# State-space input tables computed in place from turned inputs and factor rows, with their transfers begun by GpSimd

## The chip, the cores and the metric

The kernel runs as one program on one core of one Trainium2 chip. The metric is the device time of one execution in microseconds (us), and lower is better. TensorE is called PE, VectorE DVE, ScalarE ACT, GpSimd POOL and SyncE SP, as the profile does. A name such as L884 is a line of the kernel file.

## The reference

One layer of a decoder trunk is computed for 256 tokens of width 2048, in float32: a SwiGLU feed-forward block, a mixer made of a state-space part (S5) and a sparse attention part, and a second feed-forward block. The part that the change touches is the preparation of the S5 parameters:

```
dt = exp(log_dt);  lam = min(a_re, -1e-4) + i a_im
ab = exp(lam * dt)                      # one complex factor per state
co = (ab - 1) / lam                     # zero-order hold
bb = co * b                             # input matrix
x[t] = ab * x[t-1] + bb u[t]            # scan over the tokens
y[t] = Re(c x[t]) + d * u[t]
```

There are 64 groups of 16 channels with 64 states each. The kernel treats 4 tokens at a time: it needs, for every state, the products of ab^3, ab^2, ab and 1 with bb (the input table), the products of ab to ab^4 with c (the output table), and the 4 by 4 triangle of direct responses of one token to a later one (the third part of the output table). These tables depend on weights alone.

## The kernel before

The first feed-forward block (`ffn`, called with `tables`) multiplies the activations by gate and up weights in 11 blocks of 512 columns. The first five blocks (0 to 4) take both halves apart by plain products, and from block 5 on another scheme with fewer products is used (lines L523 to L525, tile `bank`). Each weight tile `raw` (128x1024, 512 KB) is loaded by SP, rounded by ACT into `hi` (L103), and the rest `lo` is formed by DVE (L105). PE then makes three products from the parts of weight and activation (`hi,ah` L278, `lo,ah` L279, `hi,al` L280), for two token tiles: 12 matmuls for one `raw`, and 192 for one half of a block. There are four `hi` and four `lo` buffers and four accumulators `acc`. A finished gate half is read by ACT (silu, L690, into `wk`), which frees its accumulators for the next half; DVE multiplies by the up half (L691).

The table work, `s5_tables`, hides beside these blocks. A list `background` holds its steps: `s5_params` (some 90 small DVE operations on 128x32 and two sines on ACT), `bias_table` (a relative-position table of the attention: ACT loads `wk<-in_rel_bias`, POOL fills it, ACT stores `rb_one` and spreads it as `rb`, 3 MB), and for each of eight channel tiles ct the steps `loads`, three `b_power`, `into`, four `c_power` and `out_of`. Function `pump` takes steps off the list as blocks go on. A scheduler then orders the instructions of every engine from these steps and their dependences, by its own estimate of times; on the chip each engine runs its row in that fixed order.

For one ct before the change: ACT begins the loads `ld` of b and c; DVE forms `bd` = co*b (L851 to L853) and three powers of it (L860 to L862); PE turns the result by 8 transposes (L322, tile `xp`, through `transpose4`), ACT copies it out (L875, tile `bt`) and begins its store to `s5in` (L876). DVE forms the powers of c in `gb` (L854, L855, L867 to L869). In `out_of` PE multiplies `bd` by `gb` (L884), DVE takes the result to `hs` (L887, L888), POOL spreads it by 16 small copies into `hz` (L892), and ACT begins the stores of `gb` and `hz` to `s5out` (L895, L896). `ld`, `bd`, `gb` and `bt` have one buffer each, so `gb` of the next ct waits until the store of this one has landed. After ct 7 the space of these tiles is given to the tiles of the second scheme, among them `sh` (written by ACT at L496), so `sh` waits for the last store of `hz`.

Of the kernel before, what the change touches and what calls it, by code (L numbers as in the profile page):

```python
# [10 lines left out]
F32 = mybir.dt.float32  # L11
F32R = mybir.dt.float32r
I32 = mybir.dt.int32
AF = mybir.ActivationFunctionType
ALU = mybir.AluOpType
# [158 lines left out]
def body(tc, a):  # L174
    nc = tc.nc
    V, S, G, T = nc.vector, nc.scalar, nc.gpsimd, nc.tensor
# [5 lines left out]
    dp = es.enter_context(tc.tile_pool(name="scratch", bufs=1, space=DRAM))  # L182
# [80 lines left out]
    background = []  # L263
# [54 lines left out]
    def transpose4(src, cols=128, n=4):  # L318
        pool = spare[0]
        p = pool.tile([128, n, 128], F32, name="xp", tag=pool.name)  # L320
        for k in range(n):
            last_transpose[0] = T.transpose(p[:, k, :], src[:, k * cols:(k + 1) * cols], ident).ins  # L322
        return p
# [296 lines left out]
    def ffn(name, rr, gen, post, last, tables=False):  # L620
# [9 lines left out]
        if tables:  # L630
            pre[0] = tc.tile_pool(name="pre", bufs=1, reuse_waits="tile")
            with tc.issue_after(stream.rounded[9]):
                s5_tables(pre[0].__enter__())
# [102 lines left out]
    ar = cp.tile([128, 32], F32, name="ar")  # L736
    ai2 = cp.tile([128, 2, 32], F32, name="ai2")
    cor = cp.tile([128, 32], F32, name="cor")
    coi2 = cp.tile([128, 2, 32], F32, name="coi2")
# [81 lines left out]
    def bc(x, ct, two):  # L821
        x = x[:, :, 4 * ct:4 * ct + 4] if two else x[:, 4 * ct:4 * ct + 4].unsqueeze(1).to_broadcast([128, 2, 4])
        return x.unsqueeze(3).to_broadcast([128, 2, 4, 32])


    in_dram = dp.tile([8, 128, 1024], F32, name="s5in")
    out_dram = dp.tile([8, 128, 1536], F32, name="s5out")

    def s5_tables(sp_):
        dsk = sp_.tile([128, 8], F32, name="dsk")  # L830
        nc.scalar.dma_start(dsk, a["ssm_d"])
        hzs = [sp_.tile([128, 4, 128], F32, name=f"hz{i}") for i in range(2)]
        for z in hzs:
            G.memset(z, 0.0)
        fold = sp_.tile([128, 32], F32, name="fold")
        V.tensor_copy(fold, ident[:, 0:32])
        for q in range(1, 4):
            V.tensor_tensor(fold, fold, ident[:, 32 * q:32 * q + 32], op=ALU.add)
        t12 = sp_.tile([128, 2, 2, 4, 32], F32, name="t12")
        t1, t2 = t12[:, 0], t12[:, 1]  # L840
        state = {}

        def loads(ct):
            for nm in ("b", "c"):
                w = sp_.tile([128, 2, 4, 32], F32, name="ld", tag="ld" + nm, bufs=1)
                nc.scalar.dma_start(w.rearrange("p r q c -> p (r q c)"), a["ssm_" + nm][ct])
                state[nm] = w
            state["bd"] = sp_.tile([128, 2, 4, 4, 32], F32, name="bd")
            state["gb"] = sp_.tile([128, 2, 4, 5, 32], F32, name="gb")
            b0, bd, gb = state["b"], state["bd"], state["gb"]  # L850
            V.tensor_tensor(t1, b0, bc(cor, ct, False), op=ALU.mult)  # L851
            V.tensor_tensor(t2, b0[:, ::-1], bc(coi2, ct, True), op=ALU.mult)
            V.tensor_tensor(bd[:, :, :, 3, :], t1, t2, op=ALU.add)  # L853
            V.tensor_copy(gb[:, 0, :, 0, :], state["c"][:, 0])  # L854
            V.tensor_scalar(gb[:, 1, :, 0, :], state["c"][:, 1], -1.0, None, op0=ALU.mult)  # L855

        def b_power(ct, j):
            bd = state["bd"]
            src = bd[:, :, :, j + 1, :]
            V.tensor_tensor(t1, src, bc(ar, ct, False), op=ALU.mult)  # L860
            V.tensor_tensor(t2, src[:, ::-1], bc(ai2, ct, True), op=ALU.mult)
            V.tensor_tensor(bd[:, :, :, j, :], t1, t2, op=ALU.add)  # L862

        def c_power(ct, k):
            gb = state["gb"]
            src = gb[:, :, :, k - 1, :]
            V.tensor_tensor(t1, src, bc(ar, ct, False), op=ALU.mult)  # L867
            V.tensor_tensor(t2, src[:, ::-1], bc(ai2, ct, True), op=ALU.mult)
            V.tensor_tensor(gb[:, :, :, k, :], t1, t2, op=ALU.subtract)  # L869

        def into(ct):
            bt = sp_.tile([128, 2, 512], F32, name="bt")
            for r in range(2):
                p = transpose4(state["bd"][:, r].rearrange("p q j c -> p (q j c)"))
                S.activation(bt[:, r], p, AF.Copy)  # L875
            nc.scalar.dma_start(in_dram[ct], bt.rearrange("p r s -> p (r s)"))  # L876

        def out_of(ct):
            bd, gb = state["bd"], state["gb"]
            hz = hzs[ct % 2]  # L880
            hp = xp.tile([128, 4, 32], F32, name="xp", tag="xp")
            for q in range(4):
                for r in range(2):
                    T.matmul(hp[32 * q:32 * q + 32], bd[:, r, q, 3, :],  # L884
                             gb[:, r, q, 0:4, :], start=r == 0, stop=r == 1, tile_position=(0, 32 * q))
            hs = sp_.tile([128, 4, 32], F32, name="hs")
            V.scalar_tensor_tensor(hs[:, 0, :], fold, dsk[:, ct:ct + 1], hp[:, 0, :], op0=ALU.mult, op1=ALU.add)  # L887
            V.tensor_copy(hs[:, 1:, :], hp[:, 1:, :])  # L888
            hq = hz.rearrange("p q (i c) -> p q i c", i=4)
            for q in range(4):  # L890
                for j in range(4):
                    G.tensor_copy(hq[32 * j:32 * j + 32, q, j:, :], hs[32 * q:32 * q + 32, 0:4 - j, :])  # L892
            od = out_dram[ct].rearrange("p (r q k) -> p r q k", r=3, q=4)
            for r in range(2):
                nc.scalar.dma_start(od[:, r], gb[:, r, :, 1:5, :].rearrange("p q k c -> p q (k c)"))  # L895
            nc.scalar.dma_start(od[:, 2], hz)  # L896

        start = stream.rounded[7]

        def at_start(f):  # L900
            with tc.issue_after(start):
                f()

        background.append(lambda: at_start(s5_params))
        background.append(bias_table)
        for ct in range(8):
            background.append(lambda ct=ct: loads(ct) if ct else at_start(lambda: loads(0)))
            for j in (2, 1, 0):
                background.append(lambda ct=ct, j=j: b_power(ct, j))
            background.append(lambda ct=ct: into(ct))  # L910
            for k in range(1, 5):
                background.append(lambda ct=ct, k=k: c_power(ct, k))
            background.append(lambda ct=ct: out_of(ct))
# [510 lines left out]
def _block_diag(x):  # L1424
    z = np.zeros((8, 2, 64, 4, 2, 16), x.dtype)
    x = x.reshape(8, 4, 2, 64, 16)
    for gp in range(2):
        z[:, gp, :, :, gp, :] = x[:, :, gp].transpose(0, 2, 1, 3)
    return z.reshape(8, 128, 4, 32)


def layout(i):
    f = {k: np.asarray(v) for k, v in i.items()}
    f = {k: (v if k in ("x", "rel_bias") else v[0]) for k, v in f.items()}
    d = {"x": np.ascontiguousarray(f["x"][0])}
# [4 lines left out]
    for n in ("ffn1", "ffn2"):  # L1440
# [3 lines left out]
    w = f["w_in"]  # L1444
    cut = np.cumsum([0, 1024, 1024] + [256] * 6 + [48, D, D])
    ssm, q, kc, vc, ks, vs, kw, vw, gn, ga, gb = (w[:, cut[j]:cut[j + 1]] for j in range(11))
    heads = [(2 * (p // 4) + hf) * 4 + p % 4 for p in range(8) for hf in range(2)]
    q = q.reshape(D, 16, 64)[:, heads].reshape(D, 1024)
# [14 lines left out]
    d["ssm_p"] = np.ascontiguousarray(np.stack([st(f["ssm_a_re"]), st(f["ssm_a_im"]), st(dt)], axis=1))  # L1463
    d["ssm_b"] = np.ascontiguousarray(np.stack(
        [_block_diag(f["ssm_b_re"]), _block_diag(f["ssm_b_im"])], axis=2)).reshape(8, 128, 256)
    d["ssm_c"] = np.ascontiguousarray(np.stack(
        [_block_diag(f["ssm_c_re"].transpose(0, 2, 1)), _block_diag(f["ssm_c_im"].transpose(0, 2, 1))],
        axis=2)).reshape(8, 128, 256)
# [20 lines left out]
```

## Time and profile before

| what | value |
|---|---|
| median of 3 runs | 2117.07 us (2113.35 to 2119.12) |
| profiled execution | 2120.92 us, its span 2119.2 us |
| PE busy | 2096.6 us (99%) |
| DVE busy | 1572.3 us (74%) |
| ACT busy | 1115.5 us (53%) |
| POOL busy | 273.3 us (13%) |
| bytes moved | 437.63 MB, mean 207 GB/s |

A busy time is the time in which at least one instruction of the engine runs; consecutive matmuls overlap, so their distance is shorter than the duration that is shown for one. The instructions that begin a transfer are not counted as busy and are shown with the name of the engine's queue (ACTq, SPq). The table work lies between about 20 and 250 us of the span.

### The profile page before, as it was taken

The numbers are of one execution on the slowest core, as the hardware profiler recorded it, in microseconds if no ns is written. First come the engines' busy times: TensorE is split into PE (matmuls) and PEld (weight loads), VectorE is DVE, ScalarE is ACT, GpSimd is POOL, SyncE is SP. The second block draws the span as 40 slices with busy tenths as digits, with TensorE's granted clock in tenths as the row PEclk, the third lists the DMA queues.
The fourth block names the chain that finished last, engine by engine and source line by source line (L and its number), as shares of the span: only waits on it lengthen the run. The fifth ranks groups of instructions, "written<-read, shape, count | busy, mean of one in ns | idle before, by whom it ended". The sixth has DMA issues, their size and how long they took to land.

```text
span 2119.2 us, 27930 instructions
## 1 busy us (share of the span) xinstructions
PE 2096.6 (99%) x10048; PEld 1726.9 (81%) x10048; DVE 1572.3 (74%) x2268; ACT 1115.5 (53%) x1537; POOL 273.3 (13%) x494
## 2 busy tenths in 40 slices
PE   8999999999999999999999999999999999999998
PEld 7887788888888878998787778888878888888886
DVE  7898788886867864454456656577898889778676
ACT  6444455555555565554445554465555555555453
POOL 1222300000000002993104320000000000000000
PEclk9999999999999999999999999999999999999999
DMA  8877656565665766567754346676556665656665
GB/s 285 268 239 234 202 196 211 197 213 180 205 206 198 272 205 225 163 223 248 276 165 139 122 144 214 203 268 184 188 191 197 208 197 190 219 170 210 217 207 179
DMA packets 137146, 437.63 MB, mean 207 GB/s; under 512 B 14880, under 2 KB 27312, under 8 KB 136880
## 3 DMA queue, kind: packets, MB, share of 16 engines
q1 hardware_dynamic: 117504, 403.10, 58.0%
q10 hardware_dynamic: 19504, 32.75, 4.5%
q8 instruction: 79, 1.29, 0.2%
q14 instruction: 59, 0.48, 0.1%
HBM read 417.42 MB, written 21.52 MB: 207 GB/s over the span
## 4 chain that ended last, share of the span: by engine, by line
PE 81%; POOL 8%; DVE 5%; issue 2%; DMA 2%; ACT 1%; ACTq 0%; DVEq 0%; SPq 0%; POOLq 0%
PE bank L524 15%; PE bank L525 15%; PE bank L523 15%; PE acc L278 10%; PE acc L279 10%; PE acc L280 10%; DVE lo L105 2%; POOL st L1005 2%; POOL sc L1002 2%; PE xp L322 2%; POOL sc L1003 1%; POOL st L1004 1%; DMA raw<-in_ffn_gu 1%; POOL hz L892 1%; DMA s5out<-gb 1%
## 5 line engine op out<-in xcount | busy, mean ns | idle before, releaser
L105 DVE TENSOR_TENSOR lo<-raw,hi 128x1024 fp32r<-128x1024 f32 (+3 forms) x676 | 796.7, 1186 | 353.7 <-ACT hi L103 352.2
L103 ACT ACTIVATE hi<-raw 128x1024 fp32r<-128x1024 f32 (+3 forms) x676 | 686.1, 1023 | 682.1 <-PE acc L280 306.8
L278 PE MATMUL acc<-hi,ah 128*128 128x512 f32 (+2 forms) x1072 | 414.9, 388 | 2.0 <-ACT hi L103 1.9
L279 PE MATMUL acc<-lo,ah 128*128 128x512 f32 (+2 forms) x1072 | 413.9, 386 | 0.0
L280 PE MATMUL acc<-hi,al 128*128 128x512 f32 (+2 forms) x1072 | 412.6, 385 | 0.0
L524 PE MATMUL bank<-lo,ah 128*128 128x512 f32 x758 | 296.7, 391 | 2.3 <-DVE lo L105 2.3
L525 PE MATMUL bank<-hi,al 128*128 128x512 f32 x746 | 290.7, 390 | 0.0
L523 PE MATMUL bank<-hi,ah 128*128 128x512 f32 x758 | 282.0, 391 | 0.0
L278 PEld LDWEIGHTS acc<-hi,ah 128*128 128x128 f32 x1072 | 201.4, 188 | 42.8 <-ACT hi L103 2.7
L279 PEld LDWEIGHTS acc<-lo,ah 128*128 128x128 f32 x1072 | 201.7, 188 | 38.9 <-issue 2.1
L280 PEld LDWEIGHTS acc<-hi,al 128*128 128x128 f32 x1072 | 201.6, 188 | 38.3 <-DVE al L351 0.3
L524 PE MATMUL bank<-lo,hT 128*128 128x512 f32 x520 | 202.5, 389 | 0.0
L525 PE MATMUL bank<-hi,hT 128*128 128x512 f32 x520 | 202.3, 389 | 0.0
L523 PE MATMUL bank<-hi,hT 128*128 128x512 f32 x520 | 190.7, 390 | 0.1
L524 PEld LDWEIGHTS bank<-lo,ah 128*128 128x128 f32 x758 | 142.4, 188 | 32.5 <-DVE lo L105 3.5
L523 PEld LDWEIGHTS bank<-hi,ah 128*128 128x128 f32 x758 | 142.3, 188 | 29.3
L525 PEld LDWEIGHTS bank<-hi,al 128*128 128x128 f32 x746 | 140.1, 188 | 28.7
L103 ACT ACTIVATE hi<-sums 128x1024 fp32r<-128x1024 f32 x84 | 88.5, 1054 | 63.0 <-DVE sums L140 29.7
L523 PEld LDWEIGHTS bank<-hi,hT 128*128 128x128 f32 x520 | 97.5, 188 | 21.1 <-ACT hi L103 0.9
L524 PEld LDWEIGHTS bank<-lo,hT 128*128 128x128 f32 x520 | 97.6, 188 | 20.2
L525 PEld LDWEIGHTS bank<-hi,hT 128*128 128x128 f32 x520 | 97.6, 188 | 20.1
L105 DVE TENSOR_TENSOR lo<-sums,hi 128x1024 fp32r<-128x1024 f32 x84 | 101.0, 1217 | 3.9 <-ACT hi L103 3.1
(322 smaller groups left out, 2674.3 us busy)
## 6 DMA issues: line engine op xcount, KB each, us to landing
raw<-in_ffn_gu SPq DMA_DIRECT2D x352, 512.0 KB, 4.3
raw<-in_ffn_d SPq DMA_DIRECT2D x176, 512.0 KB, 4.3
raw<-in_w_ya SPq DMA_DIRECT2D x64, 512.0 KB, 3.4
raw<-in_w_in SPq DMA_DIRECT2D x40, 512.0 KB, 4.1
raw<-in_w_gate_b SPq DMA_DIRECT2D x32, 512.0 KB, 3.7
raw<-in_w_out SPq DMA_DIRECT2D x32, 512.0 KB, 3.8
raw<-in_w_o SPq DMA_DIRECT2D x16, 512.0 KB, 3.9
tab<-s5out ACTq DMA_DIRECT2D x8, 768.0 KB, 6.5
```

The lines of the kernel that those rows point to most:

```text
L103: self.rounded.append(nc.scalar.activation(h, r, AF.Copy).ins)
L105: self.rest = nc.vector.tensor_tensor(l, r, h.bitcast(F32), op=ALU.subtract).ins
L278: T.matmul(o, lh, wh[:, k, :], start=kk + k == 0, stop=False)
L279: T.matmul(o, lh, wl[:, k, :], start=False, stop=False)
L280: last_product[0] = T.matmul(o, ll, wh[:, k, :], start=False, stop=kk + k == nk - 1).ins
L322: last_transpose[0] = T.transpose(p[:, k, :], src[:, k * cols:(k + 1) * cols], ident).ins
L523: T.matmul(out, lh, wh[:, j, :], start=key not in self.started, stop=False)
L524: T.matmul(out, lh, wl[:, j, :], start=False, stop=False)
L525: last_product[0] = T.matmul(out, ll, wh[:, j, :], start=False, stop=last).ins
L892: G.tensor_copy(hq[32 * j:32 * j + 32, q, j:, :], hs[32 * q:32 * q + 32, 0:4 - j, :])
L1002: G.tensor_tensor(w[:, 0], x, a4r2, op=ALU.mult)
L1005: G.tensor_tensor(y, y, w[:, 1], op=ALU.add)
```

## The change

`b_power` and the transposes of `into` go. Instead, a new step `coefs` right after `s5_params` multiplies co by ab three times (18 small DVE operations and two copies on 128x32), turns the four results by two PE transposes, and ACT copies them to three rows of 128x128 (real part, imaginary part with both signs), which POOL stores to a new DRAM tile `s5k`. A new input `ssm_bt` holds b already turned and repeated four times, so that its rows are already those of the input table. For each ct, `loads` now also loads this (`bt0`, 512 KB) and four stretches of `s5k`, each spread over 32 partitions (`kt`, 32x1536, 192 KB each). `into` is two halves of three DVE operations on 128x512: a product with the real factor, a product of the other half with the imaginary factor, and their sum. `bd` keeps only co*b, for `out_of`. All transfers of the tables (`dsk`, `ld`, `bt0`, `kt`, `s5k`, `s5in`, `s5out`) are begun by POOL instead of ACT: 11 for one ct.

```diff
     out_dram = dp.tile([8, 128, 1536], F32, name="s5out")
+    k_dram = dp.tile([128, 384], F32, name="s5k")
     def s5_tables(sp_):
         dsk = sp_.tile([128, 8], F32, name="dsk")
-        nc.scalar.dma_start(dsk, a["ssm_d"])
+        G.dma_start(dsk, a["ssm_d"])
         hzs = [sp_.tile([128, 4, 128], F32, name=f"hz{i}") for i in range(2)]
...
         state = {}
+        def coefs():
+            w = work().rearrange("p (r j c) -> p r j c", r=4, j=4)
+            k, t = w[:, 0:2], w[:, 2:4]
+            tt = V.tensor_tensor
+            V.tensor_copy(k[:, 0, 3], cor)
+            V.tensor_copy(k[:, 1, 3], coi2[:, 1])
+            for j in (2, 1, 0):
+                xr, xi = k[:, 0, j + 1], k[:, 1, j + 1]
+                tt(t[:, 0, 0], xr, ar, op=ALU.mult)
+                tt(t[:, 0, 1], xi, ai2[:, 1], op=ALU.mult)
+                tt(k[:, 0, j], t[:, 0, 0], t[:, 0, 1], op=ALU.subtract)
+                tt(t[:, 0, 2], xr, ai2[:, 1], op=ALU.mult)
+                tt(t[:, 0, 3], xi, ar, op=ALU.mult)
+                tt(k[:, 1, j], t[:, 0, 2], t[:, 0, 3], op=ALU.add)
+            p = transpose4(k.rearrange("p r j c -> p (r j c)"), n=2)
+            rows = work().rearrange("p (v s) -> p v s", v=4)
+            S.activation(rows[:, 0], p[:, 0], AF.Copy)
+            S.activation(rows[:, 1], p[:, 1], AF.Copy, scale=-1.0)
+            S.activation(rows[:, 2], p[:, 1], AF.Copy)
+            G.dma_start(k_dram, rows[:, 0:3].rearrange("p v s -> p (v s)"))
         def loads(ct):
...
                 w = sp_.tile([128, 2, 4, 32], F32, name="ld", tag="ld" + nm, bufs=1)
-                nc.scalar.dma_start(w.rearrange("p r q c -> p (r q c)"), a["ssm_" + nm][ct])
+                G.dma_start(w.rearrange("p r q c -> p (r q c)"), a["ssm_" + nm][ct])
                 state[nm] = w
-            state["bd"] = sp_.tile([128, 2, 4, 4, 32], F32, name="bd")
+            state["bd"] = sp_.tile([128, 2, 4, 32], F32, name="bd")
             state["gb"] = sp_.tile([128, 2, 4, 5, 32], F32, name="gb")
-            b0, bd, gb = state["b"], state["bd"], state["gb"]
+            state["bt"] = sp_.tile([128, 2, 4, 128], F32, name="bt0")
+            state["k"] = sp_.tile([128, 4, 3, 128], F32, name="kt")
+            G.dma_start(state["bt"].rearrange("p r q s -> p (r q s)"), a["ssm_bt"][ct])
+            for j in range(4):
+                src = k_dram[32 * j + 4 * ct:32 * j + 4 * ct + 4].rearrange("q n -> (q n)")
+                G.dma_start(state["k"][32 * j:32 * j + 32].rearrange("p q v s -> p (q v s)"),
+                                    src.unsqueeze(0).to_broadcast([32, 1536]))
+            b0, gb = state["b"], state["gb"]
             V.tensor_tensor(t1, b0, bc(cor, ct, False), op=ALU.mult)
             V.tensor_tensor(t2, b0[:, ::-1], bc(coi2, ct, True), op=ALU.mult)
-            V.tensor_tensor(bd[:, :, :, 3, :], t1, t2, op=ALU.add)
+            V.tensor_tensor(state["bd"], t1, t2, op=ALU.add)
             V.tensor_copy(gb[:, 0, :, 0, :], state["c"][:, 0])
             V.tensor_scalar(gb[:, 1, :, 0, :], state["c"][:, 1], -1.0, None, op0=ALU.mult)
-
-        def b_power(ct, j):
-            bd = state["bd"]
-            src = bd[:, :, :, j + 1, :]
-            V.tensor_tensor(t1, src, bc(ar, ct, False), op=ALU.mult)
-            V.tensor_tensor(t2, src[:, ::-1], bc(ai2, ct, True), op=ALU.mult)
-            V.tensor_tensor(bd[:, :, :, j, :], t1, t2, op=ALU.add)
         def c_power(ct, k):
...
             V.tensor_tensor(gb[:, :, :, k, :], t1, t2, op=ALU.subtract)
-        def into(ct):
-            bt = sp_.tile([128, 2, 512], F32, name="bt")
-            for r in range(2):
-                p = transpose4(state["bd"][:, r].rearrange("p q j c -> p (q j c)"))
-                S.activation(bt[:, r], p, AF.Copy)
-            nc.scalar.dma_start(in_dram[ct], bt.rearrange("p r s -> p (r s)"))
+        def into(ct, half):
+            if half == 0:
+                state["in"] = sp_.tile([128, 2, 4, 128], F32, name="bt")
+            qs = slice(2 * half, 2 * half + 2)
+            x, k, y = state["bt"], state["k"], state["in"][:, :, qs]
+            t = t12.rearrange("p a r q c -> p (a r q c)").rearrange("p (r q s) -> p r q s", r=2, q=2)
+            V.tensor_tensor(y, x[:, :, qs], k[:, qs, 0].unsqueeze(1).to_broadcast([128, 2, 2, 128]), op=ALU.mult)
+            V.tensor_tensor(t, x[:, ::-1, qs], k[:, qs, 1:3].rearrange("p q v s -> p v q s"), op=ALU.mult)
+            V.tensor_tensor(y, y, t, op=ALU.add)
+            if half:
+                G.dma_start(in_dram[ct], state["in"].rearrange("p r q s -> p (r q s)"))
         def out_of(ct):
...
                 for r in range(2):
-                    T.matmul(hp[32 * q:32 * q + 32], bd[:, r, q, 3, :],
+                    T.matmul(hp[32 * q:32 * q + 32], bd[:, r, q, :],
                              gb[:, r, q, 0:4, :], start=r == 0, stop=r == 1, tile_position=(0, 32 * q))
...
             for r in range(2):
-                nc.scalar.dma_start(od[:, r], gb[:, r, :, 1:5, :].rearrange("p q k c -> p q (k c)"))
-            nc.scalar.dma_start(od[:, 2], hz)
+                G.dma_start(od[:, r], gb[:, r, :, 1:5, :].rearrange("p q k c -> p q (k c)"))
+            G.dma_start(od[:, 2], hz)
         start = stream.rounded[7]
...
         background.append(lambda: at_start(s5_params))
+        background.append(coefs)
         background.append(bias_table)
...
             background.append(lambda ct=ct: loads(ct) if ct else at_start(lambda: loads(0)))
-            for j in (2, 1, 0):
-                background.append(lambda ct=ct, j=j: b_power(ct, j))
-            background.append(lambda ct=ct: into(ct))
+            for half in range(2):
+                background.append(lambda ct=ct, half=half: into(ct, half))
             for k in range(1, 5):
...
         [_block_diag(f["ssm_b_re"]), _block_diag(f["ssm_b_im"])], axis=2)).reshape(8, 128, 256)
+    d["ssm_bt"] = np.ascontiguousarray(np.stack([np.tile(_block_diag(f["ssm_b_" + r]).transpose(0, 3, 2, 1), (1, 4, 1, 1))
+                                                 for r in ("re", "im")], axis=2)).reshape(8, 128, 1024)
     d["ssm_c"] = np.ascontiguousarray(np.stack(
```

The scheduler puts the instructions in another order. Three places matter for what follows; line numbers in rows of the changed kernel are those of the changed file.

The first is the end of the first block. Its gate half fills `acc_153` and `acc_154` in the program before (`acc_154` and `acc_155` in the changed one), the up half follows, and the next block needs the first of these accumulators. On ACT stood before:

```order
L103 ACTIVATE hi_620<-raw_343 128x1024
L690 ACT_TABLE_LOAD
L690 ACTIVATE wk_742<-acc_153,r00_415 128x512
L930 DMA rb_one_116<-wk_574 16x384
L103 ACTIVATE hi_644<-raw_361 128x1024
L931 DMA rb_117<-rb_one_116 128x6144
L784 ACTIVATE wk_471<-wk_471 128x32
L103 ACTIVATE hi_665<-raw_457 128x1024
L785 ACTIVATE wk_471<-wk_471 128x32
L103 ACTIVATE hi_697<-raw_559 128x1024
L103 ACTIVATE hi_718<-raw_595 128x1024
L690 ACTIVATE wk_746<-acc_154,r01_428 128x512
```

and now, on the same engine, up to the transfers of the bias table (`wk_767` is the silu of the first accumulator, `xp_595` holds the two transposes of the factors):

```order
L103 ACTIVATE hi_722<-raw_560 128x1024
L103 ACTIVATE hi_743<-raw_607 128x1024
L103 ACTIVATE hi_777<-raw_643 128x1024
L862 ACTIVATE wk_598<-xp_595 128x128
L863 ACTIVATE wk_598<-xp_595 128x128
L864 ACTIVATE wk_598<-xp_595 128x128
L952 DMA wk_621<-in_rel_bias 16x32
L690 ACT_TABLE_LOAD
L690 ACTIVATE wk_767<-acc_154,r00_416 128x512
L690 ACTIVATE wk_771<-acc_155,r01_429 128x512
L960 DMA rb_one_117<-wk_622 16x384
L961 DMA rb_118<-rb_one_117 128x6144
```

The silu stood eight rows ahead of the last `hi` shown; now it stands behind all `hi` that fit into the buffers, behind the three copies of the factor rows and behind a load of the function table. The next accumulator's turn on PE was before, at the end of the up half:

```order
L278 MATMUL acc_452<-hi_644,ah1_135 128x512
L279 MATMUL acc_452<-lo_645,ah1_135 128x512
L280 MATMUL acc_452<-hi_644,al1_136 128x512
L278 MATMUL acc_750<-hi_665,ah0_133 128x512
L279 MATMUL acc_750<-lo_666,ah0_133 128x512
L280 MATMUL acc_750<-hi_665,al0_134 128x512
```

and is now:

```order
L278 MATMUL acc_453<-hi_679,ah1_136 128x512
L279 MATMUL acc_453<-lo_680,ah1_136 128x512
L280 MATMUL acc_453<-hi_679,al1_137 128x512
L322 MATMUL xp_595<-ident_75,wk_574 128x128 x2
L278 MATMUL acc_775<-hi_701,ah0_134 128x512
L279 MATMUL acc_775<-lo_702,ah0_134 128x512
```

The factors' transposes have come between the last matmul of the up half, the 192nd of the stream, and the first of the next block. On DVE, `lo_778` (the rest of `hi_777`) and 16 operations on 128x32, 12 of them of the factors, stand ahead of what these transposes read.

The second place is POOL in the course of one ct, in the changed kernel (before, its row holds the copies `hz` alone, and all of these transfers stand on ACT):

```order
L922 COPY hz_442<-hs 32x64
L922 COPY hz_442<-hs 32x32
L870 DMA ld<-in_ssm_c 128x256
L876 DMA bt_1042<-in_ssm_bt 128x1024
L879 DMA kt<-s5k 32x1536 x3
L926 DMA s5out<-hz_442 128x512
L879 DMA kt<-s5k 32x1536
L906 DMA s5in<-bt 128x1024
L925 DMA s5out<-gb 128x4x128 x2
L870 DMA ld<-in_ssm_b 128x256
```

Of the 16 copies of one ct the first 14 stand ahead of this piece. The loads of the ct after the next and the stores of the next one all stand in one row with the copies.

The third place is the end of the table work on PE. Before, the multiplication of `out_of` for ct 7 stood amid the last plain block, 69 rows ahead of the first matmul into `bank`:

```order
L279 MATMUL acc_2395<-lo_2372,ah0_133 128x512
L280 MATMUL acc_2395<-hi_2371,al0_134 128x512
L278 MATMUL acc_2395<-hi_2371,ah0_133 128x512
L884 MATMUL xp_2436<-gb_2252,bd_2251 32x128 x8
L279 MATMUL acc_2395<-lo_2372,ah0_133 128x512
L280 MATMUL acc_2395<-hi_2371,al0_134 128x512
```

and now it stands at the end of that block, right ahead of the second scheme:

```order
L279 MATMUL acc_2396<-lo_2470,ah1_136 128x512
L280 MATMUL acc_2396<-hi_2469,al1_137 128x512
L914 MATMUL xp_2159<-gb_2016,bd_2015 32x128 x8
L322 MATMUL xp_2309<-ident_75,wk_2227 128x128 x4
L322 MATMUL xp_2316<-ident_75,wk_2231 128x128 x4
L523 MATMUL bank_2567<-hi_2485,ah0_134 128x512
L524 MATMUL bank_2567<-lo_2486,ah0_134 128x512
```

The first matmul that reads `sh` comes 94 rows behind this multiplication before, and 30 rows behind it now.

## Rows read from the trace of the kernel before

**Rows 1.** Stretches: from:to, length, PE, PEld, DVE, ACT, POOL busy, clock, DMA share, GB/s.

```profile
0.00:30.00 30.00, 23.21 (x107) 18.75 (x108) 20.31 (x45) 22.66 (x50) 2.17 (x9) 1.00 0.90 323
...
53.00:106.00 53.00, 53.00 (x273) 43.42 (x271) 46.09 (x102) 24.05 (x27) 11.26 (x30) 1.00 0.83 268
...
212.00:265.00 53.00, 50.78 (x245) 41.54 (x244) 41.00 (x65) 24.70 (x31) 18.54 (x32) 1.00 0.63 202
```

**Rows 2.** PE at the end of the first block: start, duration (us), instruction.

```profile
56.34 0.39 PE L280 MATMUL acc<-hi,al 128*128 128x512 f32 x1
56.57 0.39 PE L278 MATMUL acc<-hi,ah 128*128 128x512 f32 x1
```

**Rows 3.** Groups of instructions, 53 to 265 us: busy us, mean ns, idle before (us).

```profile
L862 DVE TENSOR_TENSOR bd<-t 128x256 f32<-128x256 f32 x24 | 10.2, 423 | 0.5
...
L322 PE MATMUL xp<-ident,bd 128*128 128x128 f32 x64 | 8.3, 273 | 2.3 <-DVE bd L862 2.2
...
L496 ACT ACTIVATE sh<-wk 128x384 fp32r<-128x384 f32 x4 | 1.8, 512 | 1.0 <-DMA s5out<-hz 1.0
...
L139 DVE TENSOR_TENSOR sums<-sums,raw 128x512 f32<-128x512 f32 x2 | 1.4, 684 | 0.0
```

**Rows 4.** PE around one group of transposes.

```profile
176.59 0.39 PE L280 MATMUL acc<-hi,al 128*128 128x512 f32 x1
176.82 1.03 PE L322 MATMUL xp<-ident,bd 128*128 128x128 f32 x8
...
177.93 0.39 PE L279 MATMUL acc<-lo,ah 128*128 128x512 f32 x1
```

**Rows 5.** Waits, 53 to 265 us: total us, times, longest.

```profile
ACT hi L103 <- POOL hz L892: 16.1, 4, 8.3
DVE gb L854 <- DMA s5out<-gb: 9.5, 4, 2.6
```

**Rows 6.** ACT, from 18 to 57 us (in brackets idle time and what ended it).

```profile
18.21 0.88 ACT L350 ACTIVATE ah<-xp,gains 128x128 fp32r<-128x128 f32 x3
...
40.44 1.28 ACT L690 ACT_TABLE_LOAD   x1
41.74 0.69 ACT L690 ACTIVATE wk<-acc,r 128x512 f32<-128x512 f32 x1
...
56.82 1.06 ACT L103 ACTIVATE hi<-raw 128x1024 fp32r<-128x1024 f32 x1 [1.08 <-PE acc L280]
```

**Rows 7.** DVE, from 42 to 57 us.

```profile
42.53 0.20 DVE L758 TENSOR_SCALAR wk<-wk 128x32 f32<-128x32 f32 x1
42.77 0.20 DVE L759 TENSOR_SCALAR wk<-wk 128x32 f32<-128x32 f32 x1
...
43.93 0.19 DVE L764 SCALAR_TENSOR_TENSOR wk<-wk 128x32 f32<-128x32 f32 x1
44.04 0.18 DVE L779 TENSOR_SCALAR wk<-wk 128x32 f32<-128x32 f32 x1
...
55.44 1.22 DVE L105 TENSOR_TENSOR lo<-raw,hi 128x1024 fp32r<-128x1024 f32 x1
```

**Rows 8.** POOL's copies `hz`, four of the eight groups.

```profile
79.35 7.71 POOL L892 COPY hz<-hs 32x32 f32<-32x32 f32 x16 [35.28 <-DVE hs L887]
...
122.85 5.71 POOL L892 COPY hz<-hs 32x32 f32<-32x32 f32 x16 [15.49 <-DVE hs L887]
...
212.56 11.51 POOL L892 COPY hz<-hs 32x32 f32<-32x32 f32 x16 [17.53 <-DVE hs L887]
239.80 8.78 POOL L892 COPY hz<-hs 32x32 f32<-32x32 f32 x16 [15.74 <-DVE hs L887]
```

**Rows 9.** Transfers, 0 to 262 us: KB each, median us from issue to landing.

```profile
s5out<-gb ACTq DMA_DIRECT2D x16, 256.0 KB, 4.4
...
s5out<-hz ACTq DMA_DIRECT2D x8, 256.0 KB, 3.3
```

**Rows 10.** ACT's queue beginning a transfer.

```profile
55.55 0.35 ACTq L846 DMA_DIRECT2D ld<-in_ssm_b  x1
```

## What the change is predicted to do

> **What bounds the kernel now.** I read the busy shares first, then the stretches in which the tables are made, then the groups and waits inside them. PE is the bound: in the stretch from 53 to 106 us it is busy all the time (53.00 of 53.00 us) at the full clock, DVE 46.09 of 53 and ACT 24.05 [rows 1]. Consecutive matmuls start 0.23 us apart without a gap [rows 2]. So a step of the tables matters in three ways only: by the PE time that it takes itself, by a wait that it brings into PE's row, and in the first 30 us, where PE is busy for 23.21 us and the DMA engines are the limit (share 0.90, 323 GB/s) [rows 1]. From 212 to 265 us PE is busy 50.78 of 53: one group of transposes waits 2.2 us for DVE's `bd` [rows 1, 3]. At the end of that stretch the space of the tables is handed on, and ACT's first `sh` waits 1.0 us for the last store of `hz` [rows 3], yet no time is lost on PE there.
>
> **What goes.** The 64 transposes. Around one group of eight, the matmul before it starts at 176.59 and the second one after it at 177.93 [rows 4]: 1.34 us, less two distances of 0.23 is 0.88 us, by eight groups 7.0 us of PE. The wait of 2.2 us goes with them [rows 3]. It stems from DVE that waits for ACT, and ACT for POOL: ACT's queue held the store of `hz` behind the copies, four waits with 16.1 us in all, the longest 8.3 [rows 5]; with the stores on POOL, ACT is free of them. Together 9.2 us. That is the whole that PE can gain, since it has no other idle time here.
>
> **What costs nothing.** DVE loses 72 operations of 423 ns (30.5 us) and gets 48 on 128x512, for which the nearest row has 684 ns (32.8 us) [rows 3]. The 2.3 us more lie in eight periods, in which DVE is idle for 6.9 of 53 us [rows 1]; if that cover goes they count in the term on waits below. The 16 copies of ACT that go lie on an engine that is busy less than half of the time [rows 1].
>
> **The end of the first block.** This is the term that I hold for the surest. The next block's first matmul needs an accumulator that the silu of the gate half frees. Before, ACT did the load of its function table at 40.44 and the silu at 41.74 [rows 6], 15 us ahead of need: PE went from matmul 192 at 56.34 to 193 at 56.57 [rows 2]. Now, in ACT's row, the silu stands behind `hi_777`, three copies of the factor rows and the table load. I follow the chain with the durations of before. `hi_777` waits for the end of matmul 192; the `hi` that waits for the same matmul before starts at 56.82 and takes 1.06 [rows 6], so it is ready at 57.9. On DVE the `lo` ahead starts at 55.44 and takes 1.22 [rows 7], to 56.7; then 17 operations stand there, 15 of them on 128x32 at 0.11 us (43.93 to 44.04) or, where each needs the one before, 0.24 (42.53 to 42.77) [rows 7], and two of 128x256 at 0.42 [rows 3]: at least 2.4 us, to about 59.0. Then `lo_778`, to 60.2; 16 more of 128x32, 1.8 to 3.8 us, I take 2.4, since half of them are in independent pairs: 62.6. Two transposes, about 0.4 (eight take 1.03 [rows 4]): 63.0. Three copies as long as the 0.88 of three of the same size: 63.9; table load 1.28, silu 0.69 [rows 6]: 65.9. PE starts 9.3 us late, and I put 9.0. If DVE is ahead of its row at 57.9 and the 16 run at 0.11, it is 6.6 us; if they run at 0.24, about 10.8. What follows on ACT, the transfers of the bias table, has cover: PE has four `hi` and `lo` in its buffers, 48 matmuls or 10.9 us.
>
> **The opening.** POOL waits for nothing, so `dsk`, b, c and 512 KB of `bt0` of ct 0 are begun at about 2 us, in the stretch in which the DMA engines limit. At the full share they move 323/0.90 = 359 GB/s [rows 1]; 0.52 MB take 1.4 us, and with b and c, which also were in these 30 us but later, 2.2 us. The floor is nothing, as a tenth of the share is free. I take 1.4.
>
> **The end of the tables.** `out_of` of ct 7 now stands at the end of the last plain block on PE, and the first product with `sh` 30 rows behind: eight transposes (0.88) and 27 matmuls (6.1), 7.0 us. In that time POOL must make the 16 copies (5.71 to 11.51, for ct 7 it was 8.78 [rows 8]), the store must land (3.3 [rows 9]) and ACT must write four `sh` of 0.51 (2.0 [rows 3]): 14.1 us with 8.78. PE waits 7.1 us; with 5.71 it is 4.0, with 11.51 it is 9.8. Before, the same chain had 94 rows, over 20 us. I take 6.0, because part of DVE's and ACT's other work there will have been done ahead, and less of it slows POOL.
>
> **The waits in between.** From the first to the last group of `hz` are seven periods in 160.4 us (79.35 to 239.80 [rows 8]), 22.9 us each; without transposes and wait about 21.7. DVE is busy 87% of the period of before [rows 1], 19.9 us, and 20.3 with the new operations, so about 1 us in a period can be lost to new waits before PE feels them. POOL's row for one period holds 16 copies, 7.8 us in the mean of the eight groups, and the beginning of 11 transfers. No row shows what POOL needs to begin one. The nearest row below is ACT's 0.35 us [rows 10], by which POOL is occupied 11.7 of 21.7 us; from above nothing in the trace binds it but the whole way of a store, 3.3 us [rows 9], by which it would be 44 us. I go by the former, with a surcharge, 0.35 to 1.0, as POOL's other small steps (16 copies in 7.8 us) are 0.5 us apart. Then POOL keeps pace, but the store of `gb`, on which DVE already waited 9.5 us in four times [rows 5], ends later, as it shares a row with the loads; that wait is 0 to 2.4 us in a period, of which 1 is free. Over seven periods 0 to 10 us; I take 3.0.
>
> The Trainium skill, in "DMA: Bandwidth & Descriptors", Specifications, puts the first byte of a transfer begun by GpSimd at about 1 us, against 0.6 for one of SyncE or ScalarE. By its figures the sum would be 0.4 us higher for the store of `hz` at the end, and as much for each `gb`, which the free 1 us holds. No row before has a transfer of POOL.
>
> **The sum.** -9.2 + 9.0 + 1.4 + 6.0 + 3.0 = +10.2 us on the profiled execution's 2120.9, so 2131. That execution lies 3.9 us above the median of 2117.07; on the median it is 2127. A difference of 0.3%, 6.4 us, is about what a measurement of this kernel can tell from none.
>
> **Rivals.** *POOL becomes the pace.* If beginning a transfer costs more than (21.7 - 7.8)/11 = 1.26 us, POOL's row is longer than PE's period, the factors and the stores come later each time, and PE waits in each of seven periods. At 1.6 us it is 25.4 against 21.7, 3.7 by 7 = 26 us in place of the 3: 2150. For it speaks that the same 16 copies take 5.71 or 11.51 us [rows 8], so POOL is disturbed by something beside it; against it, that it stood idle over 15 us ahead of the groups shown [rows 8]. Chance 0.15.
>
> The Trainium skill, in "SBUF — State Buffer", Who interferes with whom, says that DVE and GpSimd share a port pair under an exclusive lock, and that transfers begun by GpSimd are held up while DVE runs two-port operations. The spread of the `hz` groups agrees with a lock of that sort and does not prove it; by the rule this rival would be the likelier, the more of DVE's operations are plain copies, and only `gb`'s first slice is one.
>
> *The losses are covered and cancel the gain.* The chain at the block's end is at its short end (6.6), the copies of ct 7 take 5.71 and `sh` 4.0 us, and the opening and the waits cost nothing: -9.2 + 10.6 = +1.4, and somewhat below nothing if PE gets late by the opening, while DVE's chain does not. About 2118. Chance 0.25.
>
> *The gain stays.* The order shows waits, but DVE runs the factors well ahead of it, since without the silu between them ACT and DVE finish the parameters sooner; the stall at the block's end falls to 2 to 3 us and the chain to `sh` is hidden: -9.2 + 3 = -6, up to -9.2. 2108 to 2111. Against it speaks that `lo_778` cannot start before matmul 192 has ended, whatever DVE does. Chance 0.12.
>
> The forecast itself, with losses between 13 and 28 us, has 0.48 and its own range is 2121 to 2136. The whole range is 2110 to 2152: below lies most of the case in which the gain stays, above POOL's pace at over 1.6 us. Faster by over 0.3% has 0.13, within it 0.29 (the case of cancelling, and the low end of the forecast), slower 0.58.
>
> **What would show it.** Right: a gap of some 9 us on PE ahead of matmul 193, ended by ACT's silu at about 66 us; no L322 on `bd`; a second gap of 4 to 10 us about 250 us, ended by `sh`, and it by the store of `hz`; PE's opening later by 1 to 2 us; beginnings of transfers on POOL's queue under 1.26 us. Wrong: a silu that ends before 58 us, a gap in every period with DVE waiting for `kt` or `gb` (then POOL is the pace), or a store of `hz` that lands within 5 us of the multiplication of ct 7.

## The result and the profile after

The changed kernel takes 2153.47 us (median of 6 runs, 2146.89 to 2155.05) against 2117.14 for the kernel before (6 runs): ratio 1.0171, 95% interval 1.0160 to 1.0181. It is slower, as forecast, but by 36 us where 10 were forecast, and 1.5 us beyond the range. The profiled execution is the fastest of the six (2146.9, span 2145.0), 26 us above the profiled one of before; the rest of the difference lies in executions without a trace. One figure of the section on the kernel before is to be mended: a half of a block has 96 matmuls, and gate and up half together the 192.

The stretches after (columns as in [rows 1]):

```profile
53.00:106.00 53.00, 45.74 (x211) 37.04 (x210) 37.84 (x97) 21.41 (x25) 14.27 (x34) 0.94 0.83 276
106.00:159.00 53.00, 49.70 (x248) 40.19 (x247) 41.50 (x72) 20.45 (x22) 33.49 (x65) 1.00 0.79 262
...
212.00:265.00 53.00, 47.95 (x218) 38.25 (x216) 42.20 (x73) 19.33 (x20) 21.10 (x47) 0.97 0.80 260
265.00:318.00 53.00, 44.95 (x199) 36.14 (x200) 42.60 (x55) 24.33 (x30) 6.88 (x19) 0.90 0.58 188
```

PE loses 7.3 us in the stretch from 53 to 106, in which it lost none before [rows 1], and goes on losing until the tables are done. The granted clock, 1.00 throughout before, falls to 0.94, 0.97 and 0.90. PE's own rows with the idle time in brackets, at the end of the first block, in mid-table and at the end:

```profile
57.61 0.39 PE L280 MATMUL acc<-hi,al 128*128 128x512 f32 x1
62.55 0.45 PE L322 MATMUL xp<-ident,wk 128*128 128x128 f32 x2 [4.55 <-DVE wk L856]
65.71 0.80 PE L278 MATMUL acc<-hi,ah 128*128 128x512 f32 x1 [2.71 <-ACT wk L690]
66.30 0.63 PE L279 MATMUL acc<-lo,ah 128*128 128x512 f32 x1
66.73 0.63 PE L280 MATMUL acc<-hi,al 128*128 128x512 f32 x1
...
69.29 0.63 PE L280 MATMUL acc<-hi,al 128*128 128x512 f32 x1
69.71 0.45 PE L278 MATMUL acc<-hi,ah 128*128 128x512 f32 x1
70.00 0.40 PE L279 MATMUL acc<-lo,ah 128*128 128x512 f32 x1
70.24 0.40 PE L280 MATMUL acc<-hi,al 128*128 128x512 f32 x1
...
157.23 0.50 PE L279 MATMUL acc<-lo,ah 128*128 128x512 f32 x1 [3.30 <-DVE lo L105]
...
225.84 0.50 PE L279 MATMUL acc<-lo,ah 128*128 128x512 f32 x1 [3.90 <-DVE lo L105]
...
267.75 1.10 PE L914 MATMUL xp<-gb,bd 128*32 128x128 f32 x16 [2.79 <-DVE gb L893]
...
282.50 0.80 PE L523 MATMUL bank<-hi,sh 128*128 128x512 f32 x1 [5.30 <-ACT sh L496]
```

Three things are to be seen. The first two gaps are the forecast one: matmul 192 starts at 57.61 (1.3 us later than in [rows 2]), and 193 at 65.71. The last is the forecast wait for `sh`. But between them stand gaps ended by DVE's `lo`, and after the first of the gaps the matmuls start 0.43 us apart (66.30, 66.73) until 69.7, then 0.23 again: half the clock, 1.2 instead of 2.4 GHz. The same follows the gaps of 3.30 and 3.90 us, with 7 to 9 matmuls at half clock each, and the one of 5.30 us, with 13 (282.5 to 288.1).

What DVE waited for, with [rows 5] to compare (us in all, times, longest):

```profile
DVE bt L902 <- issue: 9.4, 2, 5.0
DVE bt L902 <- DMA s5in<-bt: 6.7, 4, 3.0
DVE t L903 <- DMA kt<-s5k: 5.5, 1, 5.5
...
DVE gb L885 <- DMA s5out<-gb: 5.3, 3, 2.6
```

L902 and L903 are the first two products of the input table. `gb`, on which I had put the new waits, has less than before (9.5). For the 9.4 us the view names nothing that DVE waited for, but the trace shows it: the two waits end at 126.59 and 246.25, just behind the landings of the store of `bt` (`s5in<-bt`) at 126.41 and 246.07. So DVE stood 16 us for this store and 5.5 for `kt`. POOL begins the store behind the loads for the next ct:

```profile
113.25 0.53 POOL L876 DMA_DIRECT2D bt<-in_ssm_bt  x1
113.78 1.50 POOL L879 DMA_DIRECT2D kt<-s5k  x3
...
116.31 0.56 POOL L906 DMA_DIRECT2D s5in<-bt  x1
```

These landed one after the other, `bt0` at 118.3, the four `kt` from 119.5 to 124.1, the store at 126.4. DVE's row around one of the gaps, 151 to 158 us:

```profile
152.51 0.74 DVE L903 TENSOR_TENSOR t<-bt,kt 128x512 f32<-128x512 f32 x1 [5.45 <-DMA kt<-s5k]
153.18 1.27 DVE L652 TENSOR_TENSOR hT<-xp,hT 128x512 fp32r<-128x512 f32 x2
154.67 1.37 DVE L902 TENSOR_TENSOR bt<-bt,kt 128x512 f32<-128x512 f32 x2 [0.22 <-DMA s5in<-bt]
155.97 1.21 DVE L105 TENSOR_TENSOR lo<-raw,hi 128x1024 fp32r<-128x1024 f32 x1
```

DVE stands 5.45 us at L903 until `kt` has landed. The `lo` behind it ends at 157.18, and PE's gap ends at 157.23. Ahead of the gap of 3.90 us it was the store:

```profile
218.79 1.49 DVE L902 TENSOR_TENSOR bt<-bt,kt 128x512 f32<-128x512 f32 x2 [2.41 <-DMA s5in<-bt]
...
224.57 1.22 DVE L105 TENSOR_TENSOR lo<-raw,hi 128x1024 fp32r<-128x1024 f32 x1
```

Between the two, DVE did other work that was late by then, and PE's gap ended at 225.84 with this `lo`. Transfers, 60 to 290 us (KB, median us to landing), and the beginning of `kt` on POOL (ns, least, median, most):

```profile
kt<-s5k POOLq DMA_DIRECT2D x32, 192.0 KB, 7.7
s5in<-bt POOLq DMA_DIRECT2D x8, 512.0 KB, 10.6
s5out<-gb POOLq DMA_DIRECT2D x16, 256.0 KB, 7.1
```

```profile
L879 POOL DMA_DIRECT2D kt<-s5k x32: 489/498/557, 67.6 to 232.3; - x32
```

To begin one costs POOL 0.5 us, inside the bounds of the forecast and under the 1.26 at which POOL would be the pace. What grew is the way to landing: `gb` 7.1 against 4.4 [rows 9], and the store of `bt` 10.6 against 5.3:

```profile
s5in<-bt ACTq DMA_DIRECT2D x8, 512.0 KB, 5.3
```

### The profile page after: what moved, and what is told of

Read it like the earlier page. It is cut to its first block, busy times and chain, and to the rows that moved or that the text cites. A ratio compares the mean times of both kernels' runs of the same rounds, so it can differ in the third digit from the quotient of the medians.

```text
span 2145.0 us, 27875 instructions
## 1 busy us (share of the span) xinstructions
PE 2100.7 (98%) x9986; PEld 1726.9 (81%) x9986; DVE 1578.9 (74%) x2264; ACT 1110.2 (52%) x1525; POOL 321.7 (15%) x584
## 4 chain that ended last, share of the span: by engine, by line
PE 85%; DMA 4%; DVE 4%; issue 3%; POOL 2%; ACT 1%; SPq 0%; DVEq 0%; POOLq 0%; ACTq 0%
PE bank L523 16%; PE bank L524 16%; PE bank L525 15%; PE acc L278 11%; PE acc L279 11%; PE acc L280 11%; DMA s5in<-bt 2%; PE xp L322 2%; POOL hz L922 1%; DVE lo L105 1%; DMA s5out<-gb 1%; DMA raw<-in_w_in 1%; PE xp L1297 1%; PE xp L1024 1%; PE xp L1285 1%
```

## The experiments

"Before" is 2115 to 2120 us in each group of runs; ratios are to it. Theory A was that transfers begun by POOL land late; the rival B that the added bytes load the DMA engines.

**All transfers of the changed kernel on ACT; the old arithmetic with its transfers on POOL.**

```
e1_act:       G.dma_start -> nc.scalar.dma_start   in s5_tables of the changed kernel
e2_old_pool:  nc.scalar.dma_start -> G.dma_start   in s5_tables of the kernel before
```

> The changed kernel with every table transfer begun by ACT again (the new arithmetic and its 10.5 MB more of traffic kept). Theory A (transfers begun by POOL land late, 7 to 11 us instead of 3 to 5, and DVE waits for them through the single buffers bt, kt, gb): the waits in mid-table and the one for sh go, the gap of 8 us ahead of matmul 193 and its 2 us at half clock stay, 9 us of transposes and wait stay saved: 2117 to 2121 us. Rival B (the added bytes load the DMA engines, whoever begins them): landing stays at 7 us or more, the mid-table gaps stay: 2130 to 2145 us.

> The kernel before with its table transfers begun by POOL instead of ACT, the old arithmetic and the old bytes kept. Theory A: s5in and s5out land later than before and gb and bt wait for them; 3 to 12 us over before, 2120 to 2129 us. Rival B (bytes): nothing changes, 2117 us within 4 us. No gap of over 1 us ahead of matmul 193 in either.

Measured: e1 2148.50 us, 1.0154 (1.0140 to 1.0168); e2 2116.81, 0.9999 (0.9990 to 1.0007). Theory A falls from both sides: e1 keeps the loss, and e2 has none. Begun by POOL, the old stores land nearly as fast as by ACT (`bt` 5.2 against 5.3, `gb` 5.3 against 4.4), and from 50 to 300 us PE has no gap left:

```profile
s5in<-bt POOLq DMA_DIRECT2D x8, 512.0 KB, 5.2
s5out<-gb POOLq DMA_DIRECT2D x16, 256.0 KB, 5.3
```

e1 lies 3.5 us above B's range too, and B's sign failed with it: `kt` and the stores of `bt` and `gb` land in 5.9, 5.2 and 6.0 us there, not in 7 or more. With ACT the waits only change the engine. In e1 it is ACT's queue that stands among the transfers (65 to 260 us; the view names `kt`), and the `hi` behind them are late:

```profile
ACT hi L103 <- DMA kt<-s5k: 34.3, 4, 10.3
...
PE acc L278 <- ACT hi L103: 15.0, 7, 3.9
```

In the row ahead of one of these `hi`, at 109.68, the queue had begun `bt0` only at 102.56, when DVE had read its buffer, and the store of `hz` at 106.16, when POOL's copies had ended. So the loss belongs to the new way of making the table.

**The factor tiles out of the pool `work`.** The tiles of this pool are placed in the order of the program, so the silu's output had to wait for the row tile of the factors.

```
 def coefs():
-    w = work()...            rows = work()...
+    own = sp_.tile([128, 2, 4, 128], F32, name="bt")   # w, rows: its halves
```

> The changed kernel, where the two tiles of the factor step lie in the tile bt instead of the pool work, so that the silu does not have to be placed after them: in the order it comes 6 hi earlier. Theory: the gap of 7.8 us ahead of matmul 193 and 2 us at half clock go, everything else stays or gets a little worse since ct 0 is later: 2140 to 2147 us. Rival (the gap is only a wait that moves, because DVE and the tables are behind anyway and the later waits take it up): within 3 us of the changed kernel, 2150 to 2156.

> The changed kernel with both edits: all table transfers on ACT, factor tiles out of the pool work. Theory A: only the wait for sh at the end (5 us and 2 us at half clock) is left beside the saved 9 us: 2112 to 2118 us. Rival B: mid-table gaps stay, 2122 to 2135.

Measured: e3 2161.36 us, 1.0207 (1.0190 to 1.0225); e4, the same with ACT's transfers, 2149.24, 1.0155 (1.0140 to 1.0170). The gap ahead of matmul 193 is gone in both, as the theory said: in e3 PE's rows go on without idle time from 55 to 89 us. Yet e3 is slower in all: the table work starts later, and other gaps grow (5.17 us at 111.62 and 7.17 at 171.73, `lo` again; 5.26, 3.70 and 3.83 at the end). Both runs lie above every range of their expectations.

**Less, or slower, of kt.**

```
f1_kt_once:      if ct == 0: the four loads of kt
f3_kt_bt_once:   f1, and if ct == 0: the load of bt0
f2_kt_one:       four loads [32, 1536] -> one, source [4, 32 (broadcast), 1536]
f4_kt_halves:    two tiles [128, 2, 3, 128], bufs=2, one load each [4, 32, 768]
```

> The changed kernel, kt loaded for ct 0 alone and used for all ct (so seven of eight input tables hold other values). Takes away 28 transfers, 5.5 MB, and the wait for kt. Theory C (what DVE waits for in mid-table is the way of kt over DRAM, which starts only when the ct before has read the single buffer): the gaps in mid-table go, the gap ahead of matmul 193 and the one for sh stay: 2132 to 2141 us. Rival D (the operations on 128x512 themselves stand ahead of lo in DVE's row, and the transfers only look guilty): 2147 to 2156.

> As f1_kt_once, and the turned b (bt0) loaded for ct 0 alone too: no added traffic is left beside s5k. Theory C: same as f1_kt_once within 4 us, 2130 to 2141. Rival B (bytes load the DMA engines): lower than f1_kt_once by 4 us or more. Rival D: 2147 to 2156.

> The changed kernel with kt of a ct loaded by one transfer over 128 partitions in place of four over 32. Same bytes, three beginnings on POOL fewer for a ct. Theory C with the landing as its price: it lands in 5 to 7 us instead of 7.7 and more, so some of the mid-table gaps go: 2138 to 2150. If the number of transfers has no part: 2150 to 2156.

> The changed kernel with kt as two half tiles in two buffers, each loaded by one transfer over 128 partitions: the half of the next ct can start as soon as the first half of this one has been read. Theory C: 2132 to 2145 us. Rival D: 2147 to 2156.

Measured: f1 2143.92, 1.0137 (1.0122 to 1.0152); f3 2131.39, 1.0076 (1.0059 to 1.0093); f2 2237.13, 1.0575 (1.0559 to 1.0590); f4 2193.14, 1.0364 (1.0349 to 1.0380). In f1 and f3 the kernel leaves out seven of eight loads, so its tables hold other values. f2 and f4 miss by far, and tell most. One transfer for 128 partitions lands after 20.5 us, and a half of it after 11.2:

```profile
kt<-s5k POOLq DMA_DIRECT2D x7, 768.0 KB, 20.5
...
s5in<-bt POOLq DMA_DIRECT2D x6, 512.0 KB, 22.6
```

and in f2 PE then has eight gaps of 9.3 to 14.5 us, the first of them

```profile
92.97 0.80 PE L279 MATMUL acc<-lo,ah 128*128 128x512 f32 x1 [13.82 <-DVE lo L105]
```

The Trainium skill, "DMA: Bandwidth & Descriptors", Why a DMA increments its semaphore by 16 and not by 1, says that a transfer is spread over the largest number of engines up to 16 that divides its slowest dimension on both sides; here that dimension is 4, and before it was 32. The landing times agree (20.5 us for one transfer, 7.7 for each of the four with the same bytes). So the later `kt` lands (7.7, 11.2, 20.5), the longer the kernel takes (2153, 2193, 2237). In f1 `kt` is no longer waited for, but the store of `bt` is (`DVE bt L903 <- DMA s5in<-bt`, 21.4 us), and the mid-table gaps sum to 10.5 us, no less than in the changed kernel: f1 lies between the ranges of C and D and meets neither. In f3 the wait for the store is 10.1 and the mid-table gaps are under 1.8 us each. f3 lies in C's range, but 12.5 us under f1 where C allowed 4, as B had it. With less traffic the store of `bt` landed sooner: 10.6 us in the changed kernel, 7.0 in f1, 5.0 in f3.

**Order, and second buffers.** g1 makes the input table after the output table of the same ct. The others double buffers by half tiles, so that the memory stays the same.

```
g1_into_last:   c_power x4, out_of, then into(0), into(1)
k1_bt_halves:   g1; bt as [128, 2, 2, 128], bufs=2, a store for each half
k2_kt_halves:   g1; kt as [128, 2, 3, 128], bufs=2, four loads [32, 768] for each half
g3_halves:      g1 with both
```

> The changed kernel with the steps of a ct in another order: loads, the four powers of c, out_of, and only then the two halves of the input table. Nothing else differs. Theory C' (DVE stands in its row at the first product of the input table until kt, the turned b and the store of bt have landed, and the lo behind it come late): those transfers get some 8 us more, so most mid-table gaps go; out_of of ct 7 comes earlier on PE, so the wait for sh goes too: 2122 to 2136 us, with the gap ahead of matmul 193 left. Rival B (bytes): mid-table gaps as before, 2140 to 2150.

> As g1_into_last, and the input table and kt each as two half tiles in two buffers, with a store for each half and four loads over 32 partitions for each half of kt (same bytes, 5 transfers more for a ct). Theory C': the remaining waits for bt and kt get shorter: 2118 to 2132. If the number of transfers on POOL matters: over g1_into_last.

> g1_into_last with the input table bt alone as two half tiles in two buffers with a store each; kt as in the change. If the store of bt is what DVE waits for: 2125 to 2140 us. If it is kt: 2155 to 2167.

> g1_into_last with kt alone as two half tiles in two buffers, four loads over 32 partitions for each; bt as in the change. If kt's load, which starts only when the ct before has read the buffer, is what DVE waits for: 2125 to 2142 us. If it is bt: 2155 to 2167.

Measured: g1 2165.47, 1.0222 (1.0204 to 1.0240), above both of its ranges, so the order alone makes it worse; k1 2138.65, 1.0099 (1.0083 to 1.0115); k2 2138.37, 1.0094 (1.0081 to 1.0108); g3 2127.54, 1.0049 (1.0030 to 1.0068). Each second buffer takes 27 us off g1, both 38, at equal bytes. The question of which of the two it is has the answer that neither is it alone: the first products read `kt` and write `bt`. DVE's waits ahead of them, 60 to 290 us, sum to 49.0 us in g1, 25.4 in k1, 21.6 in k2 and 5.2 in g3. The windows of g3 refute B in its plain form:

```profile
110.00:160.00 50.00, 50.00 (x251) 40.76 (x250) 45.85 (x78) 21.64 (x23) 39.32 (x71) 1.00 0.95 313
160.00:210.00 50.00, 50.00 (x251) 40.81 (x250) 45.86 (x78) 20.61 (x22) 38.34 (x74) 1.00 0.92 302
```

The DMA engines are fuller than in the changed kernel (0.95 and 0.92, over 300 GB/s), and PE has no gap. D falls with it, since the 48 operations are all there. More traffic went with later landings; in these runs it was the single buffer in DVE's row that made a wait of them. In g3 two gaps are left, ahead of 193 (8.1 us in three pieces) and at `sh` (3.2).

**Everything together.**

```
g2_into_last_own, g4_halves_own:  g1, g3 with the factor tiles out of work
h1_skew:      g4; loads, c_power, out_of of ct + 1 stand ahead of kt, bt0, into of ct
h5_skew_act:  h1; ld and the stores of gb and hz on ACT
```

> As g1_into_last, and the factor tiles in bt instead of the pool work, so that the silu is placed early. Theory C': the gap ahead of matmul 193 and its 2 us at half clock go, the tables end late again (out_of of ct 7 at the end of the block) and sh costs 5 to 8 us: 2118 to 2135. Rival B: 2140 to 2160.

> g3_halves with the factor tiles out of the pool work. Theory C': no gap ahead of 193, few in mid-table, sh at the end 5 to 8 us: 2112 to 2128.

> g4_halves_own (half tiles, factor tiles out of the pool work) with the input table of a ct made after out_of of the next one, so that ct 1 does not stand behind the factors' way over DRAM and out_of of ct 7 comes 18 matmuls earlier. If the three gaps are all there is: 2110 to 2120 us; a wait for sh of 3 to 8 us may stay, since the order still puts out_of late.

> h1_skew with b, c and the stores of the output table begun by ACT as before the change, kt, bt0 and bt by POOL: 5 transfers fewer in POOL's row, out_of of ct 7 where it was in the kernel before. If the three gaps are all there is, the saved 9 us stay but for 1 to 2 of the opening: 2107 to 2113 us, under the kernel before. If ACT's row is held up by the stores: 2115 to 2130.

Measured: g2 2155.18, 1.0179 (1.0157 to 1.0201); g4 2128.79, 1.0051 (1.0036 to 1.0066); h1 2131.56, 1.0062 (1.0050 to 1.0075); h5 2142.66, 1.0111 (1.0095 to 1.0127). None comes under the kernel before. g2 lies in B's range and not in that of C', g4 0.8 us above its own. In g4 the gap ahead of 193 is gone, and two others stand at the end, 5.99 us at 252.07 and 8.41 for `sh`. h1 shows why. From 50 us on PE has no gap of 0.3 us up to 244 us, and its matmul 960, ahead of which the multiplications of `out_of` are all done in both kernels, starts 8.6 us ahead of the same one before (242.85 against 251.48): that is the saving, with the opening paid. Then it is lost at once:

```profile
246.71 0.47 PE L523 MATMUL bank<-hi,ah 128*128 128x512 f32 x1 [2.11 <-DVE hs L923]
...
267.38 0.80 PE L523 MATMUL bank<-hi,sh 128*128 128x512 f32 x1 [14.02 <-ACT sh L496]
```

```profile
ACT sh L496 <- DVE bt L909: 23.4, 1, 23.4
DVE bt L907 <- DMA kt<-s5k: 21.8, 7, 8.9
```

The waits for `kt` no longer reach PE through `lo`, but DVE still loses 21.8 us to them, the tables are done that much later, and `sh` needs their space. So "three gaps are all there is" was wrong: a gap closed in the middle came back at the end. In h5 ACT's row is held by the stores again, as the second half of its expectation says, but at 2142.66 it lies above the 2115 to 2130 named there.

## Why the prediction was right and wrong

- *What goes.* Right: no transposes of `bd`, and h1 up to matmul 960 shows the saving (8.6 us net of 1.6 for its opening, 10.2 together), 1 us more than the 9.2.
- *The end of the first block.* Right: 7.9 us (57.61 to 65.71 less one distance), forecast 9.0, ended by the silu at 65.66 as forecast (66). Two pieces were shorter than priced: the 16 small operations behind `lo` took 1.7 us (60.91 to 62.62), not 2.4, and the three copies overlap and take 0.6 (63.04 to 63.65), not 0.88. The function table and the silu took the 2.0 reckoned.
- *The opening.* Right: 1.3 us, forecast 1.4. In e2, where b and c come early but there is no `bt0`, it is 0.6, and in e1, where ACT begins `bt0` at 22.6 us, nothing (matmul 192 at 56.98 and 56.22).
- *The end of the tables.* The wait for `sh` is 5.30, forecast 6.0, by the chain that was forecast: ACT's `sh` begins when the store of `hz` has landed (280.5). From the end of the multiplication (268.85) to the last `sh` (282.44) it is 13.6 us, forecast 14.1, with 8.3 us of PE's work beside it, forecast 7.0. A second wait that I had not named stands ahead of it: `out_of` of ct 7 waits 2.79 for `gb`, since DVE is late.
- *The waits in between.* This step failed. I had it as "that wait is 0 to 2.4 us in a period", of `gb` alone, and took 3.0. The gaps there sum to 9.9 us (3.30, 3.90 and four of 0.35 to 1.24), 9.0 of them ended by `lo`, and the wait behind these is another: 16 us of DVE for the store of `bt` and 5.5 for `kt`. I had priced the 48 new operations of DVE by their duration, which was right (0.71 us against 0.684), and not by what they wait for. Before, `bt` was written by ACT, and the operations of DVE needed the loads of b and c and the store of `gb` alone; now `kt`, `bt0` and the store of `bt` end in DVE's row, in one buffer each, ahead of the `lo` that feed PE. I took a landing from stores of 256 KB that shared the queue with little else.
- *The clock.* It had no term. In the trace after, 48 matmuls are over 0.33 us from the next, most of them behind the gaps, and cost 9.4 us over their usual distance, against 1.0 before in the same stretch: +8.4. That is more than any single gap.
- The sum on the profiled execution: opening 1.3, transposes -7.0, idle time of PE 25.2 against 3.4 (+21.8), half clock +8.4, together 24.5; matmul 1060 starts 26.2 us later in the trace after. Not in these terms are the two transposes of the factors (0.45) and eight transposes at 268.78 that ran at half clock too (1.6 us to the next product, against 0.9). In the terms of the forecast it is -9.2 + 7.3 + 1.3 + 5.3 + (9.9 + 2.8) + 8.4 = 25.8, less 1.1 for a wait of before at 273.86 that went too.
- *POOL becomes the pace*, the rival nearest to the result in time, is wrong in its mechanism: 0.5 us for a beginning, and e2. Of the rule of the Trainium skill that I had put beside it ("SBUF — State Buffer", Who interferes with whom) nothing shows here: beside a DVE that is busy most of the time, no beginning of `kt` took over 557 ns. It is no test of that rule, for 12 of DVE's 233 operations from 65 to 235 us are plain copies.

What stays open: why the median lies 7 us above the profiled execution (the runs spread over 8 us, those of before over 6). The five longer executions have a mean granted clock of 0.990 to 0.992, the profiled one 0.993, so more time at half clock is a candidate; no trace shows it. It matters for the range: with the 26 us of the profiled pair alone the median would have been 2143, inside it, although the terms were wrong as said.

## What to carry to other kernels

When work moves from an engine with slack to one that feeds the bottleneck, price what its operations wait for, not how long they take: a load and a store in a single buffer, ahead of a row that must not stop, can cost their way to landing. Close such a wait with a second buffer (half tiles do it in the same memory), and follow it to the end of the stage, for a wait that no longer stops PE may only make the stage end later. A tile taken from a shared pool can hold back every later user of the pool in the schedule. And a gap on PE can have a tail: count the matmuls at half clock behind it.

## What the runs showed of the hardware

- Behind PE's gap of 7.3 us the granted clock was 0.50 from 65.7 to 69.7 us, a loss of 2.0 us; behind gaps of 3.30 and 3.90 us 7 to 9 matmuls ran at half clock (1.7 us of loss each), behind the one of 5.30 us 13 (2.8 us). Of two shorter gaps, the one of 2.22 us before the change had nothing of it (the distance stayed 0.23), and the one of 2.11 us in h1 had 7 matmuls at half clock (248.3 to 251.3).
- A beginning of a transfer takes POOL 0.50 us for `kt`, and 0.76 for a store of `gb`; ACT's queue took 0.35 for a load of b [rows 10], and in e1 0.39 for a store of `gb`.
- A load with a source of 4 by 32 repeated rows lands in 20.5 us, four loads of 32 with the same bytes in 7.7 each (medians, with the other transfers of the ct in the queue).
